# First stage of a hybrid attention and DeltaNet block: Silu's table ahead, x ahead of the bias table, two bank clears and a column sum sooner

## The chip, the cores and the metric

The kernel runs on one core of one Trainium2 chip. A core has five engines with a queue each: TensorE (PE, matrix products; its weight loads appear as PEld), VectorE (DVE), ScalarE (ACT), GpSimd (POOL) and SyncE (SP, which here issues nearly all loads). The metric is the device time of one execution in microseconds (us); lower is better. Of several executions the median is given.

## The reference

One transformer block over 1024 tokens of width 1024, in float32. A vector `c` gives shifts, scales and gates for two normalised sub-layers:

```
c_act = silu(c)
mod = c_act @ w_ada + b_ada
sh1, sc1, g1, sh2, sc2, g2 = split(mod, 6)
h = rmsnorm(x, norm_attn_g) * (1 + sc1) + sh1
proj = h @ w_in          # q,k,v for attention; q,k,v,z,b,a for the delta rule
y = concat([dilated_attention(q_a, k_a, v_a, rel_bias), gated_deltanet(...)]) @ w_out
x = x + g1 * y
h = rmsnorm(x, norm_ffn_g) * (1 + sc2) + sh2
x = x + g2 * ((silu(h @ w_gate) * (h @ w_up)) @ w_down)
return rmsnorm(x, final_norm_g)
```

The attention has three dilated branches with a bias by distance (`rel_bias`, 32 buckets by 8 heads).

## The kernel before, in words

**Precision.** Every large product is made of three products of a 32-bit format with reduced precision (fp32r): an operand is split into a rounded part (`hi`, `hh`) and the rest (`lo`, `hl`), and hi x hi, hi x lo and lo x hi are summed in a PSUM bank.

**The first stage** (lines 157 to 415) starts the projections before the norm is known. x lies transposed, in eight blocks `xts[k]` of 128 x 1024. For each block k the kernel casts and splits the weights `wf[k]` (L334 on ACT, L335 on POOL), scales the block by the column `G1[:, k]` = (1 + sc1) x norm weight and splits it (L348 on ACT, L349 on DVE), and adds its part to six PSUM banks (`first_mm`, L237). Division by the root mean square (`rs`) and the shift's contribution come later, on the sums.

`G1` itself is a product with silu(`c`). Its column 0 is made first and alone, from the 512 KB slab `wa8` (L338 to L343): 32 narrow products by `rows4` (L197, each shows as two instructions in the trace), then `by_columns`, which turns the 32-partition rows into a column on DVE (transpose at L204, then L206 or L208), then G1's column at L342. The other columns come in groups through `mod_load` and `mod_sum`: groups 0 and 1 are the rest of `G1`, groups 2 and 3 the shift `sh1`, whose sums are taken at L385 and L400.

**The bias rows.** A table `tbl` (33 x 1344, two tiles) times `rb` (the relative bias and a row of ones) gives three rows of 448 columns (L182 on PE, into banks of the tag `t`). They are evacuated with a change of sign (L184, DVE) and stored to `R_d` (L329) for the attention much later.

**PSUM.** Two banks hold the small sums: `aux` (`sums` in the trace) has `psq`, the sums of squares, in its first half and `pmod[0]`, `pmod[1]` in its second; `aux2` has `pba`, `pmod[2]` and `pmod[3]`. These parts are accumulated with `start=False`, so each has to be cleared by a DVE memset before it is used again: L341, L404, L408. Accesses to one bank are ordered among each other even where their columns differ.

**After the loop** come the root (L383, L384), the four row sums that spread it over the partitions (`rs_out`, L390 to L394), the last three blocks of each bank (`first_end`), then the shift's products with the first weights (L406, into `pmod[0]`, evacuated to `fb`) and with the gate weights (L411, into `pmod[1]`, evacuated to `fba`), and the `vd` projection (L484).

**What sets the order.** The kernel names engines and data; a scheduler at build time orders each engine's queue with a model of the times. Among instructions that are ready in the model, the one that stands first in the program goes first, so a queue can differ from the program. `urgent()` raises the rank of what it encloses. `issue_after(i)` puts what it encloses behind instruction i in i's queue, without waiting for its end. A tile of a pool takes one of the few buffers of its tag and waits until that is free: `wa8` and the modulation slabs `wm` share the tag `qk` with four buffers, `tbl` and the squares `sq` share `qd` with two, the bias rows' banks share `t` with two of the six projection banks. Waits between engines are semaphores that the scheduler adds.

**SP's queue** at the start holds, in program order: `cc`, two halves of `wa8`, `rel`, two tiles of `tbl`, `bada`, `ga`, x block 0, weights 0, modulation group 0 (four slabs), `wba`, x and weights 1 to 3, and so on.

Of the kernel before, what the change touches and what calls it, by code (L numbers as in the profile page):

```python
# [12 lines left out]
AF = mybir.ActivationFunctionType  # L13
ALU = mybir.AluOpType
# [4 lines left out]
P = 128  # L19
T = 1024  # L20
D = 1024
KT = D // P
TB = T // P
HALF = 512
# [47 lines left out]
def build(tc, I, out):  # L72
    nc = tc.nc
# [17 lines left out]
    def const(shape, name, dt=F32):  # L91
        return cp.tile(shape, dt, name=name, tag=name)

    def urgent():
        return tc.high_priority(offset=6000)
# [10 lines left out]
        out=tri, in_=tri, pattern=[[1, P]], compare_op=ALU.is_ge, fill=0.0,  # L106
# [34 lines left out]
    def tbank(name):  # L141
        return psb(name, "t", 2)
# [7 lines left out]
    def start(name, tag, shape=None, dt=F32):  # L150

        n = {"xp": 2, "qk": 4, "lu": 5, "o": 2, "VN": 2, "R": 1, "tc": TCB, "yt": 1, "os": 1, "zl": 1}.get(tag, 2)
        return (pr if tag in ("dt", "xp") else pd).tile(shape or [P, T], dt, name=name, tag=tag, bufs=n)

    cc = const([P, KT + 31], "cc")
    nc.vector.memset(cc, 0.0)
    nc.sync.dma_start(cc[:, 0:KT], I["cc"])
    nc.scalar.activation(cc[:, 0:KT], cc[:, 0:KT], AF.Silu)  # L160
# [7 lines left out]
    nc.sync.dma_start(rb[0:32, :], I["rel"])  # L168
    for t, cs in zip(tbl, (slice(0, 896), slice(896, 1344))):
        nc.sync.dma_start(t, I["tbl"][:, cs])  # L170
    bada = small("bada", [P, 48], I["bada"])
    ga = small("ga", [P, KT], I["ga"])
    mod = const([P, 48], "mod")
# [2 lines left out]
    R_d = dr.tile([8, 1344], F32, name="R_d")  # L176
    R4_d = dr.tile([8, 4, 960], F32, name="R4_d")
    Rss = []
    for j in range(3):
        n = 448  # L180
        ps = tbank(f"ps_R{j}")
        nc.tensor.matmul(ps[:8, 0:n], rb, tbl[j // 2][:, n * (j % 2) : n * (j % 2) + n], start=True, stop=True)  # L182
        Rs = start(f"Rs{j}", "tc", [8, HALF])
        nc.vector.tensor_scalar(out=Rs[:, 0:n], in0=ps[:8, 0:n], scalar1=-1.0, scalar2=None, op0=ALU.mult)  # L184
        Rss.append(Rs)
    sqs = [start(f"sq{i}", "qd") for i in range(2)]

    sh1 = const([P, KT + 31], "sh1")
    nc.vector.memset(sh1, 0.0)
# [1 line left out]
    def rows4(ps, win, w, nt, last, first=False):  # L191

        v = w.rearrange("p (t j m) -> p j t m", j=4, m=32)
        for j in range(4):
            nc.tensor.matmul(  # L197
                ps[32 * j : 32 * j + 32, 0 : 32 * nt], win, v[:, j], start=first, stop=last, skip_group_check=True
            )

    def by_columns(ps, out, nt, add=None, shape=None, tag="os"):

        t = shape or start("turned", tag, [P, 256])
        nc.vector.transpose(t[:, 0 : 32 * nt], ps[:, 0 : 32 * nt])  # L204
        if add is None:
            nc.vector.tensor_copy(out, t[:, 0 : 32 * nt : 32])  # L206
        else:
            nc.vector.tensor_tensor(out=out, in0=t[:, 0 : 32 * nt : 32], in1=add, op=ALU.add)  # L208
# [40 lines left out]
    def w_load(k):  # L249
        nc.sync.dma_start(wf[k], I["wfirst"][k])  # L250
# [5 lines left out]
    def mod_load(g):  # L256
        t0, nt = groups[g]
        for i in range(4):
            w = start(f"wm{g}_{i}", "qk", [P, 2, 128 * nt])
            nc.sync.dma_start(  # L260
                w, I["wada"][256 * i : 256 * i + 256, P * t0 : P * (t0 + nt)].rearrange("(k p) n -> p k n", p=P)
            )
            wms[g, i] = w

    def mod_sum(g):
        t0, nt = groups[g]
        ps = pmod[g]
        for k in range(KT):
            rows4(ps, cc[:, k : k + 32], wms[g, k // 2][:, k % 2], nt, k == KT - 1)
        if t0 < 8:  # L270
            by_columns(ps, sh1[:, t0 : t0 + nt], nt, bada[:, t0 : t0 + nt])
            return
        by_columns(ps, mod[:, t0 : t0 + nt], nt, bada[:, t0 : t0 + nt])
        nc.vector.scalar_tensor_tensor(
            out=G1[:, t0 - 8 : t0 - 8 + nt], in0=mod[:, t0 : t0 + nt], scalar=1.0, in1=ga[:, t0 - 8 : t0 - 8 + nt],
            op0=ALU.add, op1=ALU.mult,
        )
        scaled(t0 - 8, nt)
# [31 lines left out]
    loads = [None]  # L310

    x_load(0)
    w_load(0)
    mod_load(0)
    nc.sync.dma_start(wba, I["wba"])
    for k in range(1, 4):
# [7 lines left out]
    v_load(0)  # L324
    mod_load(3)
    v_load(1)
    for j, Rs in enumerate(Rss):
        with tc.issue_after(loads[0].ins):
            nc.sync.dma_start(R_d[:, 448 * j : 448 * j + 448], Rs[:, 0:448])  # L329
    for k in range(KT):  # L330
        wr = wf[k]
        hi = wp.tile([P, WSLOT], F32R, name=f"wh_f{k}", tag="wh", bufs=5)
        lo = wp.tile([P, WSLOT], F32R, name=f"wl_f{k}", tag="wl", bufs=5)
        nc.scalar.copy(hi[:, 0:HALF], wr)  # L334
        nc.gpsimd.tensor_tensor(out=lo[:, 0:HALF], in0=wr, in1=hi[:, 0:HALF].bitcast(F32), op=ALU.subtract)  # L335
        ws[k] = (hi, lo)
        if k == 0:
            for i in range(KT):  # L338
                rows4(pmod[1], cc[:, i : i + 32], wa8[:, i], 1, i == KT - 1)
            by_columns(pmod[1], mod[:, 8:9], 1, bada[:, 8:9])  # L340
            nc.vector.memset(pmod[1][:, 0:32], 0.0)  # L341
            nc.vector.scalar_tensor_tensor(  # L342
                out=G1[:, 0:1], in0=mod[:, 8:9], scalar=1.0, in1=ga[:, 0:1], op0=ALU.add, op1=ALU.mult  # L343
            )
            scaled(0, 1)
        for hf in range(2):
            cs = slice(hf * HALF, (hf + 1) * HALF)
            nc.scalar.mul(hh[k][:, cs], xts[k][:, cs], G1[:, k : k + 1])  # L348
            nc.vector.scalar_tensor_tensor(  # L349
                out=hl[k][:, cs], in0=xts[k][:, cs], scalar=G1[:, k : k + 1], in1=hh[k][:, cs].bitcast(F32),  # L350
                op0=ALU.mult, op1=ALU.subtract,
            )
        if k < KT - 3:
            for bank in range(6):
                first_mm(bank, k)
                if (k, bank) == (0, 3):
                    mod_sum(0)
                if (k, bank) == (3, 0):
                    mod_sum(1)
            if k > 0:  # L360
                square(2 * k - 2)
                square(2 * k - 1)
    vs = {}

    def v_slab(s, j):
# [23 lines left out]
    def rs_out(i):  # L389
# [18 lines left out]
    nc.vector.memset(pmod[1][:, 0:1], 0.0)  # L408
    for k in range(KT):
        for j in range(4):  # L410
            nc.tensor.matmul(  # L411
# [1663 lines left out]
```

## Time and profile before

| | |
|---|---|
| median of 3 runs | 1349.59 us (1348.5 to 1353.88) |
| profiled execution, its own time | 1352.06 us |
| its span, first to last instruction | 1350.3 us |
| PE busy | 1313.6 us, 97% of the span |
| DVE, ACT, POOL busy | 841.8, 619.2, 241.1 us |
| DMA traffic | 236.82 MB, mean 175 GB/s |
| first stage and `vd` projection | about the first 100 us |

The page of the profile gives totals for each engine, the span in 40 slices, DMA queues, the chain of work that ended last, and the costliest groups of instructions. Other views answer questions about a stretch of time: a timeline by engine (start, duration, engine, line, operation, output <- inputs, count, and in brackets the idle time before it and what ended it), a table of waits, a list of DMA issues, and busy times by stretch. An idle time in brackets is a wait only if there was something to do; on an engine that is not the bound it costs nothing by itself.

### The profile page before, as it was taken

The numbers are of one execution on the slowest core, as the hardware profiler recorded it, in microseconds if no ns is written. First come the engines' busy times: TensorE is split into PE (matmuls) and PEld (weight loads), VectorE is DVE, ScalarE is ACT, GpSimd is POOL, SyncE is SP. The second block draws the span as 40 slices with busy tenths as digits, with TensorE's granted clock in tenths as the row PEclk, the third lists the DMA queues.
The fourth block names the chain that finished last, engine by engine and source line by source line (L and its number), as shares of the span: only waits on it lengthen the run. The fifth ranks groups of instructions, "written<-read, shape, count | busy, mean of one in ns | idle before, by whom it ended". The sixth has DMA issues, their size and how long they took to land.

```text
span 1350.3 us, 25038 instructions
## 1 busy us (share of the span) xinstructions
PE 1313.6 (97%) x9440; PEld 1070.1 (79%) x9440; DVE 841.8 (62%) x1604; ACT 619.2 (46%) x1237; POOL 241.1 (18%) x246
## 2 busy tenths in 40 slices
PE   7999999999999999999999999999999999999997
PEld 4777787798988877667878788888888888888876
DVE  3675874556856222554379967576666775474597
ACT  3488614338332333543578333333333333454565
POOL 2334323334222433332630000000000000000000
PEclk9999999999999999999999999999999999999999
DMA  8625656457443455754544456344454665675685
GB/s 318 224 60 164 168 199 204 126 171 203 138 125 102 120 152 151 215 155 140 185 156 154 151 167 211 126 168 149 153 170 151 208 213 209 229 228 190 201 267 195
DMA packets 188520, 236.82 MB, mean 175 GB/s; under 512 B 48494, under 2 KB 96079, under 8 KB 188400
## 3 DMA queue, kind: packets, MB, share of 16 engines
q1 hardware_dynamic: 180336, 227.89, 53.0%
q10 hardware_dynamic: 8064, 7.34, 1.6%
q8 instruction: 74, 1.21, 0.4%
q14 instruction: 46, 0.38, 0.1%
HBM read 172.37 MB, written 62.92 MB: 174 GB/s over the span
## 4 chain that ended last, share of the span: by engine, by line
PE 74%; DVE 10%; DMA 6%; ACT 4%; issue 3%; POOL 2%; SPq 1%; ACTq 0%; POOLq 0%; DVEq 0%
PE wua L1666 9%; PE wga L1666 9%; PE g_a L576 6%; PE X L1866 6%; PE wuc L1666 4%; PE wgc L1666 4%; PE wo L576 4%; PE Z L1866 3%; PE g_va L602 2%; PE wgb L1666 2%; PE Y L1866 2%; PE wub L1666 2%; PE vd L484 2%; PE y L1411 1%; PE tr L1381 1%
## 5 line engine op out<-in xcount | busy, mean ns | idle before, releaser
L1656 DVE TENSOR_TENSOR wl_db<-wr_db,wh_db 128x512 fp32r<-128x512 f32 x77 | 52.8, 689 | 67.4 <-ACT wh_db L1655 67.3
L1655 ACT CAST wh_db<-wr_db 128x512 fp32r<-128x512 f32 x77 | 47.5, 621 | 87.0 <-PE X L1866 37.8
L1355 DVE CUSTOM_DVE_ANT_0 X<-S,bt 128x128 f32<-128x128 f32 (+7 forms) x64 | 30.9, 517 | 77.6 <-PE S L1350 53.2
L1866 PE MATMUL X<-wl_db,wh_da 128*128 128x512 f32 x160 | 62.5, 391 | 0.3 <-DVE wl_db L1656 0.3
L1866 PE MATMUL X<-wh_db,wh_da 128*128 128x512 f32 x160 | 62.3, 390 | 0.0
L1866 PE MATMUL X<-wh_db,wl_da 128*128 128x512 f32 x160 | 62.3, 389 | 0.0
L576 PE MATMUL wo<-yh,wh_wo 128*128 128x512 f32 x128 | 53.4, 417 | 1.6 <-DVE xo L1471 1.1
L1359 ACT ACTIVATE X<-X,sc 128x128 f32<-128x128 f32 (+7 forms) x64 | 37.0, 580 | 38.5 <-DVE sc L1355 38.4
L1656 DVE TENSOR_TENSOR wl_da<-wr_da,wh_da 128x512 fp32r<-128x512 f32 x77 | 52.7, 685 | 2.2 <-ACT wh_da L1655 2.1
L1655 ACT CAST wh_da<-wr_da 128x512 fp32r<-128x512 f32 x77 | 47.5, 617 | 12.4 <-DMA wr_da<-ao_d 6.6
L1361 POOL TENSOR_SCALAR X<-X,sc 128x128 f32<-128x128 f32 (+7 forms) x64 | 35.7, 564 | 94.8 <-DVE sc L1360 94.6
L576 PE MATMUL wo<-yl,wh_wo 128*128 128x512 f32 x128 | 51.0, 398 | 0.3 <-DVE yl L1486 0.3
L576 PE MATMUL g_a<-hh,wh_a 128*128 128x512 f32 x128 | 51.2, 400 | 0.0
L576 PE MATMUL wo<-yh,wl_wo 128*128 128x512 f32 x128 | 51.0, 399 | 0.0
L576 PE MATMUL g_a<-hl,wh_a 128*128 128x512 f32 x128 | 50.3, 393 | 0.0
L576 PE MATMUL g_a<-hh,wl_a 128*128 128x512 f32 x128 | 50.1, 391 | 0.0
L1655 ACT CAST wh_wg_s<-wg_s 128x512 fp32r<-128x512 f32 x33 | 20.6, 623 | 57.7 <-PE wuc L1666 24.4
L1655 ACT CAST wh_wu_s<-wu_s 128x512 fp32r<-128x512 f32 x33 | 20.4, 621 | 44.0 <-PE wga L1666 17.2
L1655 ACT CAST wh_wg<-wr_wg 128x512 fp32r<-128x512 f32 x31 | 19.3, 622 | 46.0 <-PE wua L1666 18.9
L602 PE MATMUL g_va<-wh_va,hh 128*128 128x256 f32 x128 | 38.3, 299 | 0.0
L602 PE MATMUL g_va<-wl_va,hh 128*128 128x256 f32 x128 | 38.1, 298 | 0.0
L602 PE MATMUL g_va<-wh_va,hl 128*128 128x256 f32 x128 | 37.9, 296 | 0.0
(551 smaller groups left out, 4155.5 us busy)
## 6 DMA issues: line engine op xcount, KB each, us to landing
wm<-in_wada SPq DMA_DIRECT2D x44, 512.0 KB, 5.3
wr_da<-ao_d SPq DMA_DIRECT2D x77, 256.0 KB, 2.8
wr_wu<-in_wu SPq DMA_DIRECT2D x50, 256.0 KB, 2.6
wr_wg<-in_wg SPq DMA_DIRECT2D x48, 256.0 KB, 2.9
ao_d<-a SPq DMA_DIRECT2D x44, 256.0 KB, 2.6
wr_wd<-in_wdn SPq DMA_DIRECT2D x44, 256.0 KB, 2.7
wr_db<-wt_d SPq DMA_DIRECT2D x44, 256.0 KB, 3.5
ao_d<-as SPq DMA_DIRECT2D x33, 256.0 KB, 2.0
```

The costliest lines, as they stand in the source:

```text
L484: nc.tensor.matmul(banks[j], a[:, w0], b[k][:, cs], start=(k == 0 and n_ == 0), stop=(k == KT - 1 and n_ == 2))
L576: last[0] = nc.tensor.matmul(ps, a[:, w0], b[k0 + k4][:, cs], start=(i == 0), stop=(i == n - 1))
L602: last[0] = nc.tensor.matmul(ps[:, :n], a[k][:, ts_], b[:, w0], start=(i == 0), stop=(i == 23))
L1355: nc.vector.tensor_tensor_reduce(out=x[:, 0:w], in0=pss[e][:, 0:w], in1=bt[:, e, 480 - w : 480], scale=1.0, scalar=3e38, op0=ALU.add, op1= ...
L1359: nc.scalar.activation(x[:, 0:w], x[:, 0:w], AF.Exp, scale=-1.0, bias=sc[:, 0:1], accum_out=sc[:, 2:3])
L1361: nc.gpsimd.tensor_scalar(out=x[:, 0:w], in0=x[:, 0:w], scalar1=sc[:, 3:4], scalar2=0.0, op0=ALU.mult, op1=ALU.add)
L1381: mm = nc.tensor.transpose(pss[e][:, i * P : i * P + P], X[e][:, cols[i] : cols[i] + P], ident)
L1411: mm = nc.tensor.matmul(yn[(slice(64 * e, 64 * e + 64), *at)], w(e), mov(e), start=(i == 0), stop=(i == len(parts) - 1), skip_group_check= ...
L1655: nc.scalar.copy(hi, src)
L1656: (eng or nc.vector).tensor_tensor(out=lo, in0=src, in1=hi.bitcast(F32), op=ALU.subtract)
L1666: nc.tensor.matmul(ps, a[:, w0], b, start=(first and k == 0 and n_ == 0), stop=(k == 3 and n_ == 2), skip_group_check=True,)
L1866: nc.tensor.matmul(bank[b], a[:, ts_], w, start=(first and n_ == 0), stop=(last and n_ == 2), skip_group_check=True,)
```

## The change

Seven edits, all in the first stage:

- An activation with Silu on a one-column tile of a constant (`silu_in`) is issued before `cc` is loaded. ACT's table for Silu is loaded with it.
- On SP's queue `rel` and `tbl` move from behind `wa8` to behind x block 0 and weights 0.
- The bias rows' products and evacuations move into the loop's block 0, behind the column `G1[:, 0]`: the products are queued behind the last product with `wa8` on PE, the evacuations behind G1's instruction on DVE. The tiles for the squares, which share buffers with `tbl`, are taken after them.
- In block 0 the clear of `pmod[1]` comes after G1's column instead of before it.
- The columns of the shift (groups 2 and 3) are turned under `urgent`.
- The clears of `pmod[0]` and `pmod[1][:, 0:1]` for the shift's products come ahead of the row sums instead of just before the products.
- The stores of the bias rows are issued after the loop in the program; they remain tied behind the last load of `vraw`.

```diff
+    silu_in = const([P, 1], "silu_in")
+    nc.scalar.activation(silu_in, eps1, AF.Silu)
     nc.vector.memset(cc, 0.0)
...
-    nc.sync.dma_start(rb[0:32, :], I["rel"])
-    for t, cs in zip(tbl, (slice(0, 896), slice(896, 1344))):
-        nc.sync.dma_start(t, I["tbl"][:, cs])
     bada = small("bada", [P, 48], I["bada"])
...
-    for j in range(3):
-        n = 448
-        ps = tbank(f"ps_R{j}")
-        nc.tensor.matmul(ps[:8, 0:n], rb, tbl[j // 2][...], start=True, stop=True)
-        Rs = start(f"Rs{j}", "tc", [8, HALF])
-        nc.vector.tensor_scalar(out=Rs[:, 0:n], in0=ps[:8, 0:n], scalar1=-1.0, ...)
-        Rss.append(Rs)
-    sqs = [start(f"sq{i}", "qd") for i in range(2)]
+
+    def bias_rows(behind):
+        for j in range(3):
+            n = 448
+            ps = tbank(f"ps_R{j}")
+            with tc.issue_after(behind[0].ins):
+                nc.tensor.matmul(ps[:8, 0:n], rb, tbl[j // 2][...], start=True, stop=True)
+            Rs = start(f"Rs{j}", "tc", [8, HALF])
+            with tc.issue_after(behind[1].ins):
+                nc.vector.tensor_scalar(out=Rs[:, 0:n], in0=ps[:8, 0:n], scalar1=-1.0, ...)
+            Rss.append(Rs)
...
         if t0 < 8:
-            by_columns(ps, sh1[:, t0 : t0 + nt], nt, bada[:, t0 : t0 + nt])
+            with urgent():
+                by_columns(ps, sh1[:, t0 : t0 + nt], nt, bada[:, t0 : t0 + nt])
             return
...
     x_load(0)
     w_load(0)
+    nc.sync.dma_start(rb[0:32, :], I["rel"])
+    for t, cs in zip(tbl, (slice(0, 896), slice(896, 1344))):
+        nc.sync.dma_start(t, I["tbl"][:, cs])
     mod_load(0)
...
-    for j, Rs in enumerate(Rss):
-        with tc.issue_after(loads[0].ins):
-            nc.sync.dma_start(R_d[:, 448 * j : 448 * j + 448], Rs[:, 0:448])
+    sqs = []
     for k in range(KT):
...
             by_columns(pmod[1], mod[:, 8:9], 1, bada[:, 8:9])
+            g1 = nc.vector.scalar_tensor_tensor(
+                out=G1[:, 0:1], in0=mod[:, 8:9], scalar=1.0, in1=ga[:, 0:1], op0=ALU.add, op1=ALU.mult
+            )
             nc.vector.memset(pmod[1][:, 0:32], 0.0)
-            nc.vector.scalar_tensor_tensor(
-                out=G1[:, 0:1], in0=mod[:, 8:9], scalar=1.0, in1=ga[:, 0:1], op0=ALU.add, op1=ALU.mult
-            )
+            bias_rows((mm, g1))
+            sqs += [start(f"sq{i}", "qd") for i in range(2)]
             scaled(0, 1)
...
+    for j, Rs in enumerate(Rss):
+        with tc.issue_after(loads[0].ins):
+            nc.sync.dma_start(R_d[:, 448 * j : 448 * j + 448], Rs[:, 0:448])
...
+    nc.vector.memset(pmod[0], 0.0)
+    nc.vector.memset(pmod[1][:, 0:1], 0.0)
     for i, bank in enumerate((2, 3, 0, 1)):
         first_end(bank)
...
-    nc.vector.memset(pmod[0], 0.0)
     for k in range(KT):
         rows4(pmod[0], sh1[:, k : k + 32], wf[k], 4, k == KT - 1)
     by_columns(pmod[0], fb, 4)
-    nc.vector.memset(pmod[1][:, 0:1], 0.0)
```

More of the change, by code (lines that the diff above doesn't have):

```diff
@@ L178, in build @@
     Rss = []
-    for j in range(3):
-        n = 448
-        ps = tbank(f"ps_R{j}")
-        nc.tensor.matmul(ps[:8, 0:n], rb, tbl[j // 2][:, n * (j % 2) : n * (j % 2) + n], start=True, stop=True)
-        Rs = start(f"Rs{j}", "tc", [8, HALF])
-        nc.vector.tensor_scalar(out=Rs[:, 0:n], in0=ps[:8, 0:n], scalar1=-1.0, scalar2=None, op0=ALU.mult)
-        Rss.append(Rs)
-    sqs = [start(f"sq{i}", "qd") for i in range(2)]
+    def bias_rows(behind):
[3 more added lines that the diff above has]
+            with tc.issue_after(behind[0].ins):
+                nc.tensor.matmul(
+                    ps[:8, 0:n], rb, tbl[j // 2][:, n * (j % 2) : n * (j % 2) + n], start=True, stop=True
+                )
+            Rs = start(f"Rs{j}", "tc", [8, HALF])
+            with tc.issue_after(behind[1].ins):
+                nc.vector.tensor_scalar(out=Rs[:, 0:n], in0=ps[:8, 0:n], scalar1=-1.0, scalar2=None, op0=ALU.mult)
+            Rss.append(Rs)
     sh1 = const([P, KT + 31], "sh1")
@@ L196, in rows4 @@
         for j in range(4):
-            nc.tensor.matmul(
+            mm = nc.tensor.matmul(
                 ps[32 * j : 32 * j + 32, 0 : 32 * nt], win, v[:, j], start=first, stop=last, skip_group_check=True
             )
+        return mm
     def by_columns(ps, out, nt, add=None, shape=None, tag="os"):
@@ L338, in build @@
             for i in range(KT):
-                rows4(pmod[1], cc[:, i : i + 32], wa8[:, i], 1, i == KT - 1)
+                mm = rows4(pmod[1], cc[:, i : i + 32], wa8[:, i], 1, i == KT - 1)
             by_columns(pmod[1], mod[:, 8:9], 1, bada[:, 8:9])
-            nc.vector.memset(pmod[1][:, 0:32], 0.0)
-            nc.vector.scalar_tensor_tensor(
+            g1 = nc.vector.scalar_tensor_tensor(
                 out=G1[:, 0:1], in0=mod[:, 8:9], scalar=1.0, in1=ga[:, 0:1], op0=ALU.add, op1=ALU.mult
             )
+            nc.vector.memset(pmod[1][:, 0:32], 0.0)
+            bias_rows((mm, g1))
+            sqs += [start(f"sq{i}", "qd") for i in range(2)]
             scaled(0, 1)
```

## The prediction, made before the result was known

> **What bounds the kernel now.** I read the page's header and engine totals first, then the waits of the tensor engine (PE), then the timeline of the first 100 us engine by engine, because the edits all lie ahead of 100 us.
>
> ```profile
> span 1350.3 us, 25038 instructions
> PE 1313.6 (97%) x9440; PEld 1070.1 (79%) x9440; DVE 841.8 (62%) x1604; ACT 619.2 (46%) x1237; POOL 241.1 (18%) x246
> ```
>
> PE is busy for 1313.6 of 1350.3 us, so it is idle for 36.7 us in all. Work on another engine counts here only if PE waits for it. What the edits could save lies in four of PE's idle times: the three at the head of the next fence and one before the modulation products at 67.89.
>
> ```profile
> 5.68 0.87 PE L197 MATMUL sums<-wa,cc 128*32 128x32 f32 x46 [5.68 <-ACT cc L160]
> 6.48 4.65 PE L182 MATMUL ps_R<-tbl,rb 33*8 33x448 f32 x6
> 11.06 0.53 PE L197 MATMUL sums<-wa,cc 128*32 128x32 f32 x18
> 12.74 0.87 PE L197 MATMUL sums<-wm,cc 128*32 128x96 f32 x16 [1.16 <-DVE sums L341]
> 13.60 0.79 PE L237 MATMUL f<-hh,wh_f 128*128 128x512 f32 x1
> 14.19 0.63 PE L237 MATMUL f<-hh,wl_f 128*128 128x512 f32 x1
> 14.61 0.63 PE L237 MATMUL f<-hh,wh_f 128*128 128x512 f32 x1
> ...
> 20.22 0.40 PE L237 MATMUL f<-hh,wl_f 128*128 128x512 f32 x1
> 20.45 0.39 PE L237 MATMUL f<-hl,wh_f 128*128 128x512 f32 x1
> ```
>
> PE's queue is in order, but not in the order of the program: the bias products (L182) stand after 46 of the 64 instructions of the first column (L197 on `wa`). The last 18 of these therefore end only at 11.6, and scale, split and first projection matmul (13.60) hang on them. PE is idle for 5.68 + 1.16 us, and its weight load waits another 0.33 us for the scaled block:
>
> ```profile
> 13.59 0.29 PEld L237 LDWEIGHTS f<-hh,wh_f 128*128 128x128 f32 x1 [0.33 <-ACT hh L348]
> ```
>
> That is 7.17 us of idle time before the projection runs; from there to 67.3 PE is idle for 0.23 us, as the first of these stretches shows (columns: length, then busy time of PE, weight loads, DVE, ACT, POOL, then granted clock, DMA share, GB/s; the second row is used further on):
>
> ```profile
> 13.60:67.30 53.70, 53.47 (x513) 37.68 (x511) 29.39 (x46) 24.23 (x37) 15.83 (x14) 1.00 0.78 289
> 73.00:101.00 28.00, 27.91 (x307) 22.95 (x308) 21.01 (x34) 26.97 (x42) 10.12 (x8) 1.00 0.17 51
> ```
>
> So the front is worth what the change takes from these 7.17 us.
>
> **The table load.** The activation table is loaded after `cc` has landed; moved ahead, it runs while `cc` is still on its way.
>
> ```profile
> 4.13 1.28 ACT L160 ACT_TABLE_LOAD   x1 [4.13 <-DMA cc<-in_cc]
> 5.42 0.21 ACT L160 ACTIVATE cc<-cc 128x8 f32<-128x8 f32 x1
> ```
>
> ACT is idle for the 4.13 us before, which hides the load and the added one-column activation (under 0.21 us, the eight-column one). Without that cover they would cost 1.28 + 0.21. `cc` is then ready at 4.13 + 0.21, and PE starts at 4.38 with the same 0.04 us between. The 64 products took 0.80 (5.68 to 6.48) and 0.53, so they end at 5.7 instead of 11.6.
>
> **The order of the loads.** On SP's queue x's first block and its weights move ahead of `rel` and the two halves of `tbl`; bada, ga, x and the weights pass three issues.
>
> ```profile
> 2.26 0.43 SPq L168 DMA_DIRECT2D rb<-in_rel  x1
> 2.74 0.77 SPq L170 DMA_DIRECT2D tbl<-in_tbl  x2
> 3.54 0.36 SPq L117 DMA_DIRECT2D bada<-in_bada  x1
> 3.94 0.43 SPq L117 DMA_DIRECT2D ga<-in_ga  x1
> 4.42 0.43 SPq L247 DMA_DIRECT2D xt<-in_xT  x1
> 4.89 0.43 SPq L250 DMA_DIRECT2D wf<-in_wfirst  x1
> 5.36 6.62 SPq L260 DMA_DIRECT2D wm<-in_wada  x4
> ```
>
> Three issues leave the front (3.54 - 2.26 = 1.28 us): x is issued at 3.14, the weights at 3.61, `rel` at 4.08, `tbl` at 4.55, and the modulation loads (L260) still at 5.36. The fourth of those waits for `wa`'s buffer until 11.6 now and will not wait afterwards; that load is not late for PE, whose order puts most of its products after the first twelve projection matmuls, so I book nothing for it.
>
> When does `tbl` land? Bytes and rates:
>
> ```profile
> 0.00:5.00 5.00, 0.00 (x0) 0.00 (x0) 1.58 (x9) 0.87 (x1) 1.84 (x13) 1.00 0.47 141
> 5.00:6.00 1.00, 0.32 (x24) 0.32 (x28) 0.00 (x0) 0.62 (x2) 0.00 (x0) 1.00 0.50 141
> 6.00:7.00 1.00, 1.00 (x43) 0.51 (x32) 0.00 (x0) 0.00 (x0) 0.00 (x0) 1.00 1.02 363
> 7.00:8.00 1.00, 1.00 (x3) 0.20 (x2) 0.00 (x0) 0.00 (x0) 0.00 (x0) 1.00 0.89 263
> ```
> ```profile
> xt<-in_xT SPq DMA_DIRECT2D x1, 512.0 KB
> wf<-in_wfirst SPq DMA_DIRECT2D x1, 256.0 KB
> tbl<-in_tbl SPq DMA_DIRECT2D x1, 115.5 KB
> tbl<-in_tbl SPq DMA_DIRECT2D x1, 57.8 KB
> bada<-in_bada SPq DMA_DIRECT2D x1, 24.0 KB, 2.5
> ```
>
> The last column of the stretches is GB/s. Up to the end of `tbl`'s first half stand `wa` (2 x 256, the same 128 x 512 block), x (512), the weights (256), bada and small ones (33) and 115.5 KB: 1429 KB, or 1.46 MB. The curve of before has moved 5 x 0.141 + 0.14 + 0.36 = 1.21 MB by 7 us and 1.47 by 8. It is at 141 GB/s from 5 to 6, where x's issue at 4.42 has not yet brought data; with x 1.28 us earlier I estimate that this slice runs at the 363 of the next, which saves 0.6 us: the bytes are through at 7.4 instead of 8.0. Landing comes later than the byte count: bada's bytes (ahead of them `wa`, `rel`, `tbl`) are 0.73 MB, through at about 5.2, and it lands at 3.54 + 2.5 = 6.0, 0.8 later. So `tbl` lands near 8.2. Bounds: not before 4.55 + 2.5 = 7.05, and 8.8 with the old curve.
>
> **Bias products behind the first column.** They now cannot hold up the column. By the same curve x lands about 1.0 us and the weights 0.3 us before `tbl`, and each then passes ACT once (scaling, cast); so the first projection matmul is ready at about the same time as the bias products, a little later. These stand ahead of it in the program, so I put them first in the queue. From the first of them to the next instruction they took 11.06 - 6.48 = 4.58 us.
>
> The projection then starts near 8.2 + 4.6 = 12.8, not 13.6. But as the 16 modulation products that now fill the gap before 13.60 still have to run, I count idle time, not the start: 4.38 before the first product, 8.2 - 5.7 = 2.5 for `tbl`, in all 6.9 against 7.17. **Front: 0.3 us gained**, by the bounds of `tbl` from 1.4 gained (7.05) to 0.3 lost (8.8). I take the value at 8.2 because both of its parts, curve and lag, come from rows of this queue. The evacuations of the bias rows (L184) now queue on DVE behind G1; what stands behind them is the residual part of the split, which the projection needs only after the bias products that they follow. The clearing of the bank, moved behind G1, takes one small instruction out of DVE's chain, inside the 2.5 us. Two moves I book at nothing: the squares take `tbl`'s buffers and so still follow the bias products, but PE needs the first square only after the second block's matmuls; and the stores of the bias rows, now traced after the loop, stay tied behind the last of the `vraw` loads on SP, so nothing else on that queue changes places with them.
>
> **The clock.** Projection matmuls start 0.42 us apart at 14.19 and 14.61, and 0.23 apart at 20.22 and 20.45, while the granted clock of the stretches is 1.00 throughout. The 4.58 us of bias products, 8 columns wide, did not bring the faster pace. The Trainium skill, "TensorE: Matmul & The Clock Gate", Part 1, has PE at half clock until it has been busy for about 3.4 us. By that rule alone the bias products should have warmed it here; the trace does not agree for so narrow a product. I keep the slow stretch as long as it is and price the other outcome as a rival.
>
> **Sums and clears further on.** `urgent` on the shift's columns lets the transpose at L204 go ahead of queued bank evacuations on DVE; the clears at L404 and L408 go ahead of the row sums' copies.
>
> ```profile
> 67.89 1.95 PE L197 MATMUL sums<-wf,sh 128*32 128x128 f32 x64 [0.55 <-DVE sh L208]
> ...
> 73.09 0.73 PE L411 MATMUL sums<-sh,wba 128*32 128x1 f32 x64 [1.42 <-DVE sums L408]
> ...
> 102.32 0.50 PE L576 MATMUL g_qd<-hl,wh_qd 128*128 128x512 f32 x1 [0.72 <-POOL hl L464]
> ```
>
> Both waits can go whole: 0.55 + 1.42 = 1.97 us. The clears cost two memsets that DVE does earlier, in the stretch up to 67.3, where it is busy for 29.39 of 53.70 us and PE has projection matmuls queued; without that cover they would hold up the row sums by their own length. But what is late next is ACT:
>
> ```profile
> 88.23 1.34 ACT L500 ACTIVATE xp_v<-xp_v,fbv 128x512 f32<-128x512 f32 x2 [0.37 <-DVE fbv L206]
> ...
> 91.27 0.82 ACT L461 ACTIVATE hh<-xt,sh,G 128x512 fp32r<-128x512 f32 x1 [0.48 <-PE vd L484]
> ```
>
> From 73 to 101 us ACT is busy for 26.97 of 28.00 us. It can move forward only by its two short waits, 0.37 + 0.48 = 0.85, and by what `fb` moves, 0 to 0.55. PE already waits at 102.32 for blocks that ACT prepares, so of 1.97 us only 0.85 to 1.4 survive. **I take 1.1**, the middle, since `fb` sits between a transpose that moves and DVE work that does not.
>
> **Sum.** 0.3 + 1.1 = 1.4 us. The profiled execution took 1352.06 us, 1.76 of them outside the span; it becomes 1350.7. The runs shown have a median of 1349.59 (1348.5 to 1353.88), 2.47 below it; the same 1.4 off the median gives 1348.2 us.
>
> **Rivals.** (1) *Bias products among or behind the projection matmuls.* Ready times of 8.2 and 8.5 are close, and the order is made from a model, not from these times. Against it: they come first in the program. At the fast pace (0.23 against 0.42) they would take 2.5 of their 4.58, so 2.1 us more are gained: 1346.1. (2) *The clock rises sooner*, since bias products and projection now run without the gap of 1.16 us: the twelve matmuls of the first four banks gain 0.19 each, 2.3 us: 1345.9. That is what the skill's rule would give; for it speaks the missing gap, against it the slow pace at 13.60 after 4.58 busy us. (3) *The removed wait comes back in full:* PE gets to the products of the gate rows early, and `fb` and the later casts do not move: only the 0.3 of the front remain, 1349.3, as if the change had hardly been made. (4) *Slower: `tbl` lands late.* It is small but behind 768 KB more than before, and every matmul of PE now queues behind products that wait for it in order. Each us after 8.5 is a us lost at the front; from 9.6 on it eats the 1.1 as well. Landing at 11.2 gives 1351.2. Against it: nothing large stands ahead of it but x and the weights, and the four modulation loads are issued after it.
>
> **How the numbers follow.** Forecast 0.50; rival 1 0.20, rival 2 0.08, rival 3 0.12, rival 4 0.10. The range holds forecast and rivals 1 to 3 with their bounds: rival 1 with 1.4 of the front and 1.4 further on is 1349.59 - 4.9 = 1344.7, less 1.1 for the spread from median to lowest run, 1343.6; the upper end is rival 4's 1351.2. An effect under 0.5% (6.7 us) is about what a measurement of this kernel can't tell from none. Only rivals 1 and 2 together with both upper bounds come near it, or a new order of instructions in later stages, which the trace cannot show: faster 0.06. Slower by that much needs `tbl` beyond 16 us or such a new order: 0.04. The rest is 0.90.
>
> **What would show it.** In the profile after: the table load near 1.2 and `cc` at 4.35; the column's products done by 5.8; bias products from about 8.2 in one piece; the first L237 matmul near 12.8; no wait for DVE at the shift products and L411; a longer wait for POOL's `hl` at L576, 1.3 instead of 0.72. I am wrong if projection matmuls stand before the bias products, if PE reaches the fast pace less than 4 us after its first L237, or if the saved 1.97 us is still there after L576.

## The result, and the profile after

The changed kernel has a median of 1355.2 us (21 runs, 1351.07 to 1365.79) against 1349.82 us (21 runs, 1346.28 to 1355.71) for the kernel before on the same chip: ratio 1.0054, interval 1.0034 to 1.0074. It is slower by 4.6 to 10.0 us, where 1.4 us of gain had been forecast. Eight of its 21 runs, the profiled one among them (1365.79 us, mean granted clock 0.988; that of before: 1352.06, 0.996), had a clock of 0.992 or less and took 1360.93 us or more; the other thirteen had 0.995 or more and took at most 1355.84.

The header and PE's total of the page after:

```profile
span 1364.1 us, 25039 instructions
PE 1327.4 (97%) x9440; PEld 1077.8 (79%) x9440; DVE 841.9 (62%) x1604; ACT 619.3 (45%) x1238; POOL 244.3 (18%) x246
```

PE does the same 9440 products and is busy 13.8 us longer, exactly what the span grew by. Its idle time is the same 36.7 us. So little of the loss is waiting; the same work ran more slowly.

**The front.** PE's queue after (timeline: start, length, engine, line, operation, names, count, idle time before and what ended it):

```profile
3.94 0.66 PE L201 MATMUL sums<-wa,cc 128*32 128x32 f32 x32 [3.94 <-ACT cc L162]
5.17 0.65 PE L201 MATMUL sums<-wa,cc 128*32 128x32 f32 x32 [0.57 <-DMA wa<-in_wa]
10.49 0.80 PE L242 MATMUL f<-hh,wh_f 128*128 128x512 f32 x1 [4.67 <-ACT wh_f L341]
11.94 0.80 PE L242 MATMUL f<-hh,wl_f 128*128 128x512 f32 x1 [0.66 <-POOL wl_f L342]
12.66 4.65 PE L184 MATMUL ps_R<-tbl,rb 33*8 33x448 f32 x6
17.24 0.79 PE L242 MATMUL f<-hl,wh_f 128*128 128x512 f32 x1
17.83 0.63 PE L242 MATMUL f<-hh,wh_f 128*128 128x512 f32 x1
18.26 0.63 PE L242 MATMUL f<-hh,wl_f 128*128 128x512 f32 x1
```

The column is done at 5.8, as intended. But two projection products stand ahead of the bias products. They wait for x, its scaling and the cast of the weights, and the bias products wait behind them until 12.66, though their loads, issued in the same order in e3 below, were in by 9.2 there. The products behind still start 0.43 us apart at 18 us. ACT shows the same delay, first in the kernel after:

```profile
8.59 1.33 ACT L357 ACTIVATE hh<-xt,G 128x512 fp32r<-128x512 f32 x2 [4.71 <-DMA xt<-in_xT]
...
24.75 1.95 ACT L357 ACTIVATE hh<-xt,G 128x512 fp32r<-128x512 f32 x3 [5.84 <-DVE G L280]
```

The scaling of x's second block in the kernel before:

```profile
20.73 1.34 ACT L348 ACTIVATE hh<-xt,G 128x512 fp32r<-128x512 f32 x2 [6.57 <-DVE G L274]
```

The front lost 4.0 us. At the shift's products and at the wait for `hl` the kernel after stands so:

```profile
71.95 1.95 PE L201 MATMUL sums<-wf,sh 128*32 128x128 f32 x64 [0.55 <-DVE sh L213]
74.73 0.71 PE L423 MATMUL sums<-sh,wba 128*32 128x1 f32 x64
...
104.84 0.50 PE L588 MATMUL g_qd<-hl,wh_qd 128*128 128x512 f32 x1 [0.71 <-POOL hl L476]
```

Against before's 67.89, 73.09 and 102.32 it is late by 4.06, 1.64 and 2.52 us. The wait of 1.42 us is gone and the 0.55 has stayed. The 1.64 shows more gain than there is: between the two groups of `sums` products seven projection products stood before and three stand now, 0.23 us each, and the four that are missing follow behind. So 2.5 us of a loss of 13.8 are there at 105 us.

**Behind the first stage** the order of the instructions of every engine is the same in both programs, and PE's n-th product can be set beside PE's n-th. The lag of a start behind the same start of before, in us (the kernels e4, e7, e9 and e10 are told below; before's profile was itself 2.2 us above its median):

| at (us, before) | after | e4 | e7 | e9 | e10 |
|---|---|---|---|---|---|
| 20 | 4.0 | -2.5 | -1.3 | 2.7 | -0.6 |
| 100 | 2.5 | -5.1 | -1.3 | 1.2 | -3.2 |
| 380 | 2.4 | -7.5 | -3.7 | -2.5 | -5.4 |
| 420 | 10.1 | -1.1 | -2.9 | -2.8 | -6.1 |
| 820 | 8.4 | -1.9 | -1.8 | -4.8 | -7.6 |
| 1140 | 11.6 | 1.3 | 1.4 | -4.8 | -7.6 |
| last | 13.7 | 1.4 | 2.1 | -4.4 | -7.7 |

After loses 7.6 us in one step near 390 and 3.2 us evenly from 820 to 1140. The even loss first. One stretch of 100 us in the gate and up products (length; busy us and instructions of PE, weight loads, DVE, ACT, POOL; granted clock, DMA share, GB/s), and two groups of products in it (busy us, mean ns, idle before), kernel before:

```profile
900.00:1000.00 100.00, 100.00 (x443) 82.86 (x442) 70.52 (x112) 37.10 (x64) 0.00 (x0) 1.00 0.50 171
```
```profile
L1666 PE MATMUL wga<-H11h,wh_wg 128*128 128x512 f32 x12 | 4.7, 390 | 0.0
...
L1666 PE MATMUL wga<-T4h,wh_wg 128*128 128x512 f32 x12 | 4.7, 389 | 0.0
```

The same in the kernel after:

```profile
900.00:1000.00 100.00, 100.00 (x438) 81.94 (x437) 70.31 (x112) 35.75 (x62) 0.00 (x0) 1.00 0.51 167
```
```profile
L1678 PE MATMUL wga<-H11h,wh_wg 128*128 128x512 f32 x12 | 4.8, 396 | 0.0
...
L1678 PE MATMUL wga<-T4h,wh_wg 128*128 128x512 f32 x8 | 3.1, 389 | 0.0
```

PE is busy throughout at a clock of 1.00 and yet does 5 products fewer in 100 us. Only the products that read `H11` and `H21`, 24 of every 84, (and the few of `T2` directly behind) are slower. Over 1344 products from about 825 us on the starts lie 229.05 ns apart instead of 226.67; behind a product that reads one of the two the next starts 232 to 234 ns later, by the mean of each tile, instead of 227. With the first gate group near 720 us that is 3.9 us.

The step near 390, kernel before, then after:

```profile
381.69 0.37 SPq L899 DMA_DIRECT2D tn<-tn_d  x1
386.15 1.78 DVE L927 STREAM_TRANSPOSE U<-tn 32x256 f32<-32x256 f32 x4 [7.09 <-DMA tn<-tn_d]
...
388.87 0.21 PE L938 MATMUL lv<-cs,U 32*32 32x32 f32 x1 [0.75 <-DVE cs L934]
```
```profile
383.88 0.37 SPq L911 DMA_DIRECT2D tn<-tn_d  x1
...
389.04 1.20 PE L934 MATMUL lv<-tn,dt 32*32 32x32 f32 x64 [0.38 <-DMA tn<-tn_d]
389.09 1.78 DVE L939 STREAM_TRANSPOSE U<-tn 32x256 f32<-32x256 f32 x4 [7.87 <-DMA tn<-tn_d]
...
391.81 0.26 PE L950 MATMUL lv<-cs,U 32*32 32x32 f32 x1 [0.79 <-DVE cs L946]
```
```profile
385.00:391.00 6.00, 5.62 (x113) 5.12 (x111) 1.85 (x5) 1.26 (x5) 0.85 (x1) 1.00 1.19 243
391.80:408.90 17.10, 17.09 (x219) 15.01 (x220) 6.51 (x14) 4.61 (x12) 2.21 (x3) 0.50 0.24 74
```

Two things differ. The load of `tn` (128 partitions, rows of 128 bytes) takes 5.16 us from its issue to its first use instead of 4.46, so that PE waits 0.38 us ahead of the narrow `lv` products. And behind the second wait, 0.79 us for `cs`, the granted clock is 0.50 for 17.1 us, while PE is busy for 17.09 of them. The kernel before has nearly the same second wait (0.75) and no such stretch there.

**What the two have in common.** The change adds one tile, `silu_in`, of one 4-byte word in each partition. The allocation of the built program gives it 32 bytes in the pool of the constants, and every tile allocated behind it on that side of SBUF lies 32 bytes off its place before, seen in multiples of 256: `H11` at byte 9504 of its partition instead of 9472 (which is 37 x 256), `H21` and `tn` likewise. The tiles on the other side, `T2` and `T4` and the weights among them, stay where they were.

### The profile page after: what moved, and what is told of

Its sections match the earlier page's. It is cut to its first block, busy times and chain, and to the rows that moved or that the text cites. A ratio compares the mean times of both kernels' runs of the same rounds, so it can differ in the third digit from the quotient of the medians.

```text
span 1364.1 us, 25039 instructions
## 1 busy us (share of the span) xinstructions
PE 1327.4 (97%) x9440; PEld 1077.8 (79%) x9440; DVE 841.9 (62%) x1604; ACT 619.3 (45%) x1238; POOL 244.3 (18%) x246
```

## The experiments

Three theories of the loss were on record. ORDER: the front's order costs it. LATER (with LOADS for the order of the loads): the front's end only changes what happens later. ADDRESS, formed after the first four runs: the 32 bytes cost it. Ratios are to runs of the kernel before on the same chip, each with its 95% interval.

**e1_sums**: before, with the columns under `urgent` and the earlier clears, nothing else.

> The kernel before with only the sums of the change: the shift's columns turned under urgent, the two clears ahead of the row sums. Three theories on the loss of 5.4 us. ORDER: it arises in PE's queue before 24 us, where two projection matmuls now stand ahead of the bias products, wait for x, cast and split, and hold the bias products and all that follows back by 4.0 us; the sums give back 1.5 (at the wait for hl, 102.32 before, 104.84 after). LOADS: x, its weights and the table land too late in their new order on SP. LATER: it arises after 105 us, where the granted clock is at half for longer in the profile after (17 us near 392 us). ORDER and LOADS expect the same here: L411 without a wait for DVE, the wait for hl near 100.9 instead of 102.32, median 1.4 us below before, 0.999. LATER, if the clears or the urgent sums are to blame: a share of runs above 1360 us as in the kernel after (8 of 21), and a median not below before.

1347.34 us, ratio 0.9995 (0.9975 to 1.0016). No loss, and a gain too small to tell. The wait at the gate rows fell from 1.42 to 0.57 us.

**e2_front**: after, with these two edits undone.

> The kernel after with the sums undone (no urgent on the shift's columns, clears where they were): the front of the change alone. ORDER and LOADS: the scaling of block 1 starts near 24.7 us (20.73 before), and the wait for hl comes near 106.3 us; median 4 to 5 us above before, 1.003 to 1.004, so above the kernel after without its slow runs. LATER, if it is the front that brings the long stretch at half clock: again about a third of the runs above 1360 us.

1356.66 us, 1.0055 (1.0035 to 1.0076). All of the loss is in the front's edits, to which the Silu's tile belongs, and it is there although none of the six runs had a clock of 0.993 or less. Its scaling of block 1 came at 23.75, 3.0 us late; the same 229.05 ns in the gate products.

**e3_bias_first**: after, with block 0's projection queued behind the last bias product.

```diff
-                first_mm(bank, k)
+                with tc.issue_after(last_bias.ins) if k == 0 else ExitStack():
+                    first_mm(bank, k)
```

> The kernel after with the first block's projection matmuls queued on PE behind the last bias product; loads as in the kernel after. ORDER: the bias products start near 8.2 us in one piece, the first projection matmul near 12.8, the scaling of block 1 near 20.4 (24.75 after, 20.73 before); with the sums the median is 1.5 to 2 us below before, 0.9985 to 0.999. LOADS: the table lands no sooner than x's 8.6 us plus the weights, so the bias products start at 9.5 or later and the projection near 14.1; the front stays 0.5 us or more behind before and the median is 1 us below before at most. LATER: the front's order makes no difference to the runs above 1360 us.

1353.77 us, 1.0066 (1.0037 to 1.0094). From the timelines of PE's weight loads, PE and ACT:

```profile
9.20 0.12 PEld L184 LDWEIGHTS ps_R<-tbl,rb 33*8 33x8 f32 x2 [3.84 <-DMA tbl<-in_tbl]
```
```profile
9.23 4.63 PE L184 MATMUL ps_R<-tbl,rb 33*8 33x448 f32 x6 [3.73 <-DMA rb<-in_rel]
13.79 0.79 PE L243 MATMUL f<-hh,wh_f 128*128 128x512 f32 x1
```
```profile
21.10 1.34 ACT L358 ACTIVATE hh<-xt,G 128x512 fp32r<-128x512 f32 x2 [4.27 <-DVE G L281]
```

The order was worth 3.65 us at the front (24.75 to 21.10), so ORDER holds there. That is one execution of each; in e2 and e9, which have the order of the kernel after, the front was 3.0 and 2.7 us late instead of 4.0, so about 1 us of the 3.65 may be the execution's. What the products then wait for is put down to `rel`, a load of 1 KB, and that of their first weights to `tbl`: both are in by 9.2. And the total is still as slow as the kernel after: the front is not the whole loss.

**e4_tbl_ahead**: e3 with `rel` and `tbl` loaded ahead of `bada` again.

```diff
     wa8 ...
+    nc.sync.dma_start(rb[0:32, :], I["rel"])
+    for t, cs in zip(tbl, (slice(0, 896), slice(896, 1344))):
+        nc.sync.dma_start(t, I["tbl"][:, cs])
     bada = small("bada", [P, 48], I["bada"])
```

> As the kernel with the projection behind the bias products, but the loads of rel and the table back where they were, ahead of bada and of x: bias products behind the whole first column, table early. ORDER: the bias products follow the column at 5.8 us, end at 10.4, and the projection starts between 10.4 and 11.5 (x and its weights land 1.3 us later than in the kernel after, near 9.9, and are cast by 10.6 to 11.2); the scaling of block 1 near 18.5; with the sums the median is 3.5 us below before, 0.9975. LOADS: x and the weights, not the order, are what the front waits for, so the projection starts no sooner than 12.5 and the median is within 2 us of before.

1352.21 us, 1.0025 (1.0002 to 1.0048), although its front is 2.5 us earlier than before's:

```profile
5.69 4.65 PE L187 MATMUL ps_R<-tbl,rb 33*8 33x448 f32 x6
10.42 1.65 PE L246 MATMUL f<-hh,wh_f 128*128 128x512 f32 x3
```
```profile
18.27 1.34 ACT L358 ACTIVATE hh<-xt,G 128x512 fp32r<-128x512 f32 x2 [6.93 <-DVE G L284]
```

Against e3, from which it differs only in the place of `rel` and `tbl` on SP's queue, the front is 2.8 us earlier (18.27 against 21.10): moving these loads behind x cost that much. In the table of lags it is 7.5 us ahead at 380 and loses 6.3 near 390 and 3.2 from 820 to 1140, like after. This took the theory from the front to the addresses.

**e7_shift32**: before, with an unused tile of one word. No instruction is added or moved.

```diff
     cc = const([P, KT + 31], "cc")
+    const([P, 1], "spare")
```

> The kernel before with one unused tile of one word beside cc, which takes 32 bytes of each partition and moves every tile that is allocated behind it in that pool's side of SBUF by 32 bytes (H11, H21 and tn among them); no instruction is added, removed or moved. Theory ADDRESS (what the change loses behind its first stage comes from the scratch tile silu_in, which shifts those tiles by 32 bytes): the gate and up products that read H11 and H21 start 234 to 235 ns apart instead of 227, the mean between 820 and 1125 us is 229.05 ns instead of 226.67, which with the first gate group is 3.9 us; the load of tn takes 5.1 to 5.2 us from its issue to its first use instead of 4.45 to 4.5; half-clock stretches near 385 us come in some executions; in all slower than before by 3.9 us or more, ratio 1.003 to 1.007. Theory LATER (the front's end only moves the start of the granted clock's stretches) and theory ORDER (all of it is the order at the front): the same as before, ratio 0.999 to 1.001, 226.67 ns and 4.5 us.

1354.67 us, 1.0048 (1.0024 to 1.0072). An unused tile alone costs as much as the whole change. Its stretch, its groups and its `tn` are those of after:

```profile
900.00:1000.00 100.00, 100.00 (x439) 81.92 (x438) 69.64 (x110) 37.15 (x64) 0.00 (x0) 1.00 0.51 171
```
```profile
378.07 0.37 SPq L900 DMA_DIRECT2D tn<-tn_d  x1
...
383.19 1.20 PE L923 MATMUL lv<-tn,dt 32*32 32x32 f32 x64 [0.64 <-DMA tn<-tn_d]
```

The load takes 5.12 us, the gate products stand 229.05 ns apart. Its nine runs with a clock above 0.993 have a median of 1352.3 us, the 31 such runs of before beside it 1348.1: 4.2 us are lost without the low clock, near the 3.9 us of the gate and up products and the 0.64 us wait for `tn` together. ADDRESS held, ORDER and LATER fell as theories of the whole.

**e9_after_unmoved**: after, its scratch word in the second word of `eps1`'s 32 bytes. Against before, some tiles change buffers with each other, all by multiples of 256 bytes; seen in multiples of 256 nothing moves in SBUF.

```diff
-    eps1 = const([P, 1], "eps1")
+    eps2 = const([P, 2], "eps1")
+    eps1 = eps2[:, 0:1]
...
-    silu_in = const([P, 1], "silu_in")
-    nc.scalar.activation(silu_in, eps1, AF.Silu)
+    nc.scalar.activation(eps2[:, 1:2], eps1, AF.Silu)
```

> The kernel after with its scratch word put into the second word of eps1's 32 bytes instead of a tile of its own, so that no tile of SBUF lies elsewhere than before; every instruction stays where after has it. Theory ADDRESS: the pace between 820 and 1125 us is 226.67 ns, tn's load takes 4.45 to 4.5 us, and what is left is the front, 4.0 us late at the scaling of block 1 and 2.5 us at 100 us: ratio 1.000 to 1.003, and executions with a clock of 0.993 or less become as rare as in before (7 of 61) instead of 8 of 21. Theory LATER (the late front alone brings the low clock on): a third or more of the executions stay at 0.993 or less, ratio 1.002 to 1.005.

1347.69 us, 1.0006 (0.9993 to 1.0019); no run of 12 at a clock of 0.993 or less, nor any of the 29 of before beside it.

```profile
900.00:1000.00 100.00, 100.00 (x443) 82.81 (x442) 68.01 (x107) 37.49 (x65) 0.00 (x0) 1.00 0.51 169
```
```profile
378.94 0.37 SPq L911 DMA_DIRECT2D tn<-tn_d  x1
383.40 1.79 DVE L939 STREAM_TRANSPOSE U<-tn 32x256 f32<-32x256 f32 x4 [7.09 <-DMA tn<-tn_d]
```

443 products again, `tn` after 4.46 us. The two halves of the loss add up, within intervals of 0.0013 to 0.0024 either way: 0.0048 for the place and 0.0006 for all seven edits without it make the 0.0054 measured.

**e5_preload** and **e11_preload_unmoved**: before with the Silu ahead and nothing else, on a tile of its own and in `eps1`'s second word.

> The kernel before with the Silu on a scratch tile put ahead of cc's load, and nothing else of the change. The front should come out earlier by 0 to 1.3 us (cc ready at about 4.4 instead of 5.4, the products of column 1 sooner, x and wh_f as before). Theory ADDRESS: the same losses as with the unused tile, 3.9 us and the longer load of tn, so before plus 2.5 to 4, ratio 1.002 to 1.005. Theories LATER and ORDER: same as before or faster by up to 1 us, ratio 0.999 to 1.001.

> The kernel before with the Silu put ahead on eps1's second word: only the preload, no move in SBUF. Theory ADDRESS: e5_preload's 1.4 us ahead at the scaling of block 1 and 2 us at 100 us reach the end: before minus 1 to 2.5 us, ratio 0.998 to 0.9995. Theory LATER: as e5_preload, ratio 1.001 to 1.005.

1.0029 (1.0008 to 1.0050) and 1.0002 (0.9986 to 1.0018). The preload loses only through its tile; by itself it gains nothing that can be told in the total, though in e11's profile PE starts at 4.42 us and the scaling of block 1 comes at 19.57, 1.2 us earlier than before.

**e6_pad64** and **e8_front_pad**: after and e4 with a scratch tile of 64 bytes.

> The kernel after with the scratch tile made 64 bytes long instead of 4, so that what lies behind it moves by 64 bytes instead of 32; no instruction's place changes. Theory ADDRESS: the first stage stays 4.0 us late at the scaling of block 1 and about 2.5 us late at 100 us, the pace between 820 and 1125 us goes back to 226.67 ns, tn's load to 4.5 us, and the stretches of half clock near 390 us go: before plus 2 to 3 us, ratio 1.001 to 1.003. Theory LATER: as the kernel after, ratio 1.004 to 1.007, pace 229 ns.

> The kernel of e4_tbl_ahead (after, with rel and tbl loaded ahead of bada and the first block's projection queued behind the last bias product) with the scratch tile made 64 bytes long. Theory ADDRESS: the 2.5 us ahead of before at the scaling of block 1 and the 5 us ahead at 100 us now survive to the end, since neither the pace of the gate products nor the load of tn changes: before minus 4 to 6 us, ratio 0.995 to 0.997. Theory LATER: as e4_tbl_ahead, ratio 1.000 to 1.005.

1.0050 (1.0026 to 1.0074) and 0.9985 (0.9964 to 1.0005). Both missed: I had taken 64 bytes for harmless. The gate products still stand 228.1 ns apart and `tn` takes 5.1 to 5.2 us.

**e12_shift128** and **e14_shift256**: before with an unused tile of 128 and of 256 bytes.

> The kernel before with an unused tile of 128 bytes where e7_shift32 had one of 4 bytes (32 taken): H11, H21 and tn move by 128 bytes. If what counts is that a row begins on a multiple of 128 bytes: the same as before, 226.67 ns, tn's load 4.5 us, ratio 0.999 to 1.001. If a multiple of 256 is wanted: part of the loss that 64 bytes gave, 227 to 228 ns, ratio 1.001 to 1.003.

> The kernel before with an unused tile of 256 bytes: every tile behind it starts 256 bytes further. If what counts is the place of a row modulo 256 bytes: 226.67 ns, tn's load 4.5 us, the same time as before, ratio 0.999 to 1.001. If any other place than before's costs: 227.5 ns or more and 1.001 to 1.004.

1.0025 (1.0008 to 1.0041) and 1.0001 (0.9973 to 1.0029). With 128 bytes `tn` takes 4.50 us again but the products stand 228.65 ns apart; with 256 they are at 226.67 and `tn` at 4.50. So for these products the place counts modulo 256 bytes, for this load 128 is enough.

**e10_front_unmoved**: e4 with the scratch word in `eps1`; **e15_front_nosums**: the same without the two edits of e1.

> The kernel of e4_tbl_ahead (rel and tbl ahead of bada, projection behind the bias products) with the scratch word in eps1's second word, so that nothing moves in SBUF. Theory ADDRESS: the 2.5 us ahead at the scaling of block 1, grown to 5 at 100 us, reach the end, with 226.67 ns in the gate products: before minus 4 to 8 us, ratio 0.994 to 0.997. Theory LATER: the gain is lost to the clock in the middle as in e4_tbl_ahead, ratio 0.998 to 1.003.

> The kernel of e10_front_unmoved without the sums put ahead on VectorE and without the earlier clearing of the banks. Theory ADDRESS with the front's order: the wait for the sums of 1.42 us at the shift products and 0.55 us ahead of them are back, of which 1.0 us was worth keeping: 1 us above e10_front_unmoved, before minus 2 to 5 us, ratio 0.996 to 0.999. If the sums are worth nothing once the front is early: as e10_front_unmoved, 0.9968 within 0.001.

1342.71 us, 0.9968 (0.9956 to 0.9979), and 1345.16 us, 0.9968 (0.9944 to 0.9992). Both beat the kernel before by 0.3%. PE in e10 has the bias products in the hole that x leaves:

```profile
4.91 0.66 PE L205 MATMUL sums<-wa,cc 128*32 128x32 f32 x32 [0.33 <-DMA wa<-in_wa]
5.61 4.63 PE L187 MATMUL ps_R<-tbl,rb 33*8 33x448 f32 x6
10.42 1.65 PE L246 MATMUL f<-hh,wh_f 128*128 128x512 f32 x3 [0.18 <-ACT wh_f L342]
```

The sums show at 100 us, where e10 is 2.2 us ahead of e15, but the ratios do not tell the two apart. e15's wait is the one that the clears remove:

```profile
71.59 0.71 PE L424 MATMUL sums<-sh,wba 128*32 128x1 f32 x64 [1.14 <-DVE sums L421]
```

**e13_tn_late, e16_tn_five, e17_tn_six**: e9 with the load of `tn` issued in four, five and six parts one behind the other, to delay it with nothing moved.

> The kernel of e9_after_unmoved (after, with nothing moved in SBUF) whose load of tn is issued in four parts one behind the other, so that the last part lands later, as the moved tn did; the pace of the gate products stays 226.67 ns. Theory WAIT (the late tn makes TensorE wait ahead of the narrow lv products, and that gap is what lets the granted clock fall there): a wait for DMA tn of 0.2 to 0.6 us comes back at the first lv, a stretch of half clock of 10 to 17 us starts near 385 us in some executions, and a third of the executions have a clock of 0.993 or less (4 of 12); ratio 1.000 to 1.004. Theory CHANCE (the low clock comes by itself in the kernels that move tn): the same wait and no such stretch, at most 1 of 12 executions at 0.993 or less, ratio 0.999 to 1.002, as e9_after_unmoved.

> As e13_tn_late with five parts instead of four: each part added 0.65 us of issue there and the last landed 4.67 us after the first issue, so here about 5.3 us after it, against 5.16 in the kernel after and 4.46 in e9_after_unmoved, and a wait for DMA tn of 0.2 to 0.5 us stands ahead of the first lv. Theory WAIT: 3 or more of the executions at a clock of 0.993 or less, or a stretch of half clock of 10 to 17 us near 385 us in the profile; ratio 1.000 to 1.004. Theory CHANCE: at most 1 such execution, no such stretch, ratio 0.999 to 1.002.

> As e16_tn_five with six parts: the last lands about 5.9 us after the first issue and the wait ahead of the first lv is 0.8 to 1.1 us. Theory WAIT: the low clock as often as there or more often, 3 or more executions at 0.993 or less, ratio 1.001 to 1.005. Theory CHANCE: at most 1, and the added wait alone, ratio 0.999 to 1.002.

0.9996 (0.9974 to 1.0019), 1.0012 (0.9988 to 1.0036) and 1.0023 (0.9995 to 1.0050). In four parts `tn` came 4.67 us after the first issue, which PE's queue still covered, and no run of 12 had a clock of 0.993 or less. In five and six parts four of 12 had, each. In e16 `tn` came after 4.91 us, in e17 after 5.36, both earlier than I had worked out. The expected wait ahead of the first `lv` did not come in either; in e17 that for `cs` behind it grew to 0.97 us (0.48 in e9), and the half clock followed, 391.2 to 408.3:

```profile
382.79 3.27 SPq L913 DMA_DIRECT2D tn<-tn_d  x6
...
388.15 1.78 DVE L944 STREAM_TRANSPOSE U<-tn 32x256 f32<-32x256 f32 x4 [7.97 <-DMA tn<-tn_d]
...
390.87 0.21 PE L955 MATMUL lv<-cs,U 32*32 32x32 f32 x1 [0.97 <-DVE cs L951]
```
```profile
391.20:408.30 17.10, 17.10 (x212) 15.01 (x202) 6.21 (x14) 4.14 (x11) 2.21 (x3) 0.50 0.23 74
```

Over all runs a clock of 0.993 or less came in 32 of 96 executions of the eight kernels whose `tn` is moved by 32 or 64 bytes, in 8 of 24 with `tn` late in five or six parts, in 9 of 90 of the kernels with `tn` in time, and in 14 of 141 of the kernel before. That speaks for the late `tn` as what brings the clock down, but it is not shown. Beside e16 and e17 the kernel before had 4 of 23, so their 8 of 24 can be chance. The profile of e16 has its half clock elsewhere. And of the eight kernels with `tn` moved only after, e3, e4 and e6 show the stretch near 390 in their profile; the other four have the same two waits, 0.28 to 0.64 and 0.8 us, without it.

## Why the prediction was wrong, point by point

**The step that failed** is the one on the table load: "ACT is idle for the 4.13 us before, which hides the load and the added one-column activation." The instruction was costed in time and its output tile was not costed at all. Its 32 bytes alone measured +0.0048 (e7), some 6.5 us. Of these, 3.9 are the gate and up products, by the traces; the rest, with an interval of about 3 us either way, fits the wait for `tn` and the low clock. Why the clock falls stays open. The paragraph on the chances allowed for a loss in later stages only by "a new order of instructions", at 0.04; the order stayed, the places changed. None of the rivals had this. An effect of 0.5% was also held to be about what can't be told from none; the interval of the change itself reaches 0.2% either way.

**The table load** itself ran as predicted or better: load at 0.81, `cc` ready at 3.9 (predicted 4.35), column done at 5.8 (5.7). By itself it was worth 1.2 us at the front of one profile and nothing that could be told in the total (e11).

**The order of the bias products** failed too: "These stand ahead of it in the program, so I put them first in the queue." The scheduler put two projection products ahead. That is rival 1's order, but with the other sign: priced at 2.1 us of gain because the bias products would run at the fast pace, it cost 4.0 us, because they stayed slow (4.58 us from the first to the next instruction, as before) and the free time from 5.8 to 10.49 went unused. e3 shows the price of PE's order, up to 3.65 us, and e4 against e3 that of the loads' order, 2.8 us.

**The landing of `tbl`** near 8.2, the hinge of rival 4, did not decide in after, where PE waits for x's scaling and cast. In e3, where the bias products do wait for their loads, `rel` and `tbl` were in at 9.2, 1.0 us later than forecast. x was used at 8.59, as soon as it had landed, where the prediction had it land about 1.0 us before `tbl`, at 7.2.

**Sums and clears**: 1.1 predicted of 1.97. In after 1.5 us survive at 105 us (4.06 late before, 2.52 behind). The split was not the predicted one: the 1.42 went whole, the 0.55 stayed, and the wait for `hl` is 0.71 as before, not 1.3. In the total this part could not be told from nothing (e1; e10 against e15).

**The clock's pace at the front** was kept slow rightly: the starts at 17.83 and 18.26 are 0.43 us apart behind 4.58 us of bias products. Rival 2 did not come.

**What is left without the move** is e9's 1.0006, that is -0.9 to +2.6 us, where 1.4 us of gain was forecast. Rival 3's 0.3 us of gain lies inside the interval, the forecast just outside.

## What to carry to other kernels

A new tile, even one that nothing reads, moves all that is allocated behind it, so price it by where it puts the large operands: here they want starts at multiples of 256 bytes, and a scratch word belongs in the hole of a tile that exists. When an edit loses far from where it was made, count the same products in the same 100 us of both profiles, and time the old kernel with nothing but the new allocation in it. Where an instruction is to fill a hole, tie its place in the queue, since a scheduler's model need not see the hole.

## What the runs showed of the hardware that was not expected

- Behind a 128x512 fp32r product whose streamed operand starts 32 bytes off a multiple of 256 the next product starts 232 to 234 ns later on average instead of 227, at a granted clock of 1.00. The mean over the gate and up products, a part of which read such an operand: 226.67 ns at offsets 0 and 256, 229.05 at 32, 228.1 at 64, 228.65 at 128.
- The load of `tn` in rows of 128 bytes takes 5.1 to 5.2 us to its first use with a place 32 or 64 bytes off, 4.4 to 4.5 at offsets 0, 128 and 256.
- The granted clock falls to 0.50 for 3.4, 6.8, 13.7 or 17.1 us at a time (in e16 once for 34.1), multiples of 3.4. The Trainium skill, "TensorE: Matmul & The Clock Gate", Part 1, gives half clock as the state after an idle window of about 3.4 us. The length fits; such an idle window is not in this trace: from 385 to 391 PE was busy for 5.62 of 6.00 us, and its longest idle time ahead of the stretch at 391.8 was 0.79.
